# A hybrid mixer and mixture-of-experts step on one core: the first shift and scale from eight slabs of whole rows, x loaded first

## The chip, the cores and the metric

The kernel runs on one core of a Trainium2 chip. The core has TensorE (PE, matrix products), VectorE (DVE), ScalarE (ACT), GpSimd (POOL) and SyncE (SP, here used to start DMA transfers). The engines run on their own and wait for each other by semaphores. On-chip data lie in SBUF (128 partitions); TensorE writes into eight banks of PSUM. Weights come from device memory through 16 DMA engines, which serve queues that SP, ACT and POOL fill. The metric is the device time of one execution in microseconds (us); the runs of the kernel before gave 1415.63, 1417.6 and 1422.11 us, median 1417.6.

## The reference, cut to what matters

Two groups of 128 tokens (context and denoising sample, 1024 channels) go through one layer with shared weights. All in float32.

```python
mod = silu(cond) @ w_mod + b_mod                 # per group; six parts of 1024: sh1, sc1, g1, sh2, sc2, g2
h = rmsnorm(x) * norm1_g * (1 + sc1) + sh1       # first shift and scale; x_sample has pos added first
z = h @ w_in + b_in                              # 20 column slabs of 256: Fourier, conv a, conv b, S5, 3 gates
br_f = fourier_mix(z_f) @ w_four
br_c = silu(layernorm(depthwise_conv31(z_a * sigmoid(z_b)))) @ w_conv_out
br_s = glu(gelu(s5_scan_both_directions(z_s))) @ w_ssm_out
x = x + g1 * ((gate_f * br_f + gate_c * br_c + gate_s * br_s) @ w_out)
x = x + g2 * top4_of_32_experts(rmsnorm(x) * norm2_g * (1 + sc2) + sh2)
y = rmsnorm(x) * final_norm_g
```

The outputs are y for both groups and the final S5 states. The S5 parameters (lam, dt, B, C) are made into tables of complex powers first; the scan then goes over 16 chunks.

## The kernel before, in words

The weights come in slabs of 1 MB ([128, 2048] float32). A ring (class Ring, line 169) has a list of slabs in the order in which they are wanted and a list of free slots; when a slab is done with, its slot is given back and the next load is written into SP's queue (give and pump, lines 179 to 189). Slots 0 to 3 go round like this in the first part; slots 6 to 9 are dropped after their first use (line 440), because they become S5 tables.

The order of all instructions up to the router is made when the program is built: some thirty generators (line 1364) each yield one operation or the name of a flag that they wait for, and a planner (class Sched, line 55) always takes the operation that could start first by its own table of costs, plus 0.2 us for each point in PRIO. Each engine then runs its instructions in the order in which they were handed out. An in-order queue so can hold up work that is ready behind work that is not; this holds for SP's loads too. The planner's costs know nothing of two engines that slow each other.

The first shift and scale are made in four blocks of 256 channels. A slab m0 of this part (line 350) has all 1024 input rows of 256 output columns, of the shift or of the scale, so its rows in memory are 1 KB long; two slabs make a block. first_mod (line 497) multiplies the two conditions (cs, padded to 32 columns) with a slab, eight input chunks over four row groups of a bank, two chunks to each group. modulate (line 517) copies each block's bank out to R0, turns it by four transposes into PSUM, sums the four row groups (vsum, line 528), adds b_mod (line 529), makes (1 + sc1) * norm1_g (line 531), and applies both to xT, the transposed normalized x: on ScalarE rounded to hhi (line 536), on VectorE in full (line 538) and the rest as hlo (line 539). Each block sets flags hmod0 to hmod7 for the channels done.

Around it run: s5_params, s5_inputs and powers (VectorE steps on 128x32 pieces, from lam and dt; flags lam, Bb, pw0); b_transposes (from ssm_b_re and ssm_b_im, for Bb); first_norm (line 547, from X and pos); tables_in (line 803, 24 steps of 128x1024 for four tables T0 to T3, shared out between VectorE and POOL, from Bb and pw0); m1_transposes (line 810, the tables turned into slots 6 to 9); columns_in (line 442, seven late parameter loads on SP, begun at flag R0); splitter (line 1063, each weight slab in four pieces, ScalarE rounds, VectorE or POOL subtracts); main_products (line 1099, three products per pair, from flag m0 and hmod), two banks in turn; evacuate (line 1157, which waits for flag M11 before it writes the first S5 columns, since they share a table's buffer). The S5 scan (line 880) follows the tables, and the convolution's 31 taps (line 989) the eighth column slab. The expert stage loads 12 slabs for each of 32 experts through 20 slots.

The loads at the start stand at lines 420 to 440. "Y" is SP's queue, "S" ScalarE's, "G" POOL's.

Of the kernel before, what the change touches and what calls it, by code (L numbers as in the profile page):

```python
# [9 lines left out]
F32 = mybir.dt.float32  # L10
# [195 lines left out]
def build(tc, A, O):  # L206
# [3 lines left out]
    with es:  # L210
# [40 lines left out]
        def dma(e, dst, src):  # L251
            n = 1
            for d in dst.shape:
                n *= d
            return sch.op(f"{e}{n * 4 / 3.6e5:.3f}", 1.0 if e == "G" else 0.05, [dst] if local(dst) else [],
                          [src] if local(src) else [], lambda: ENG[e].dma_start(dst, src))
# [4 lines left out]
        def tr(out, in_):  # L261
            return sch.op("P", 0.107 * in_.shape[0] / 128, [out], [in_], lambda: te.transpose(out, in_, ident[:in_.shape[0], :in_.shape[0]]))  # L262

        def mm(out, lhsT, rhs, start, stop=False):
            n, m = size(rhs), lhsT.shape[1]
            if lhsT.dtype != F32:
                c = max(n, m) * 4.17e-4
            elif m > 64:
                c = max(n, m) * 1.667e-3
            else:  # L270
                c = n * 1.667e-3 / (4 if m <= 32 else 2) + 0.0145
            return sch.op("P", c, [out], [lhsT, rhs],
                          lambda: te.matmul(out, lhsT, rhs, start=start, stop=stop, skip_group_check=True))  # L273
# [10 lines left out]
        def stt(o, a, sc, b, op0=OP.mult, op1=OP.add, e="V"):  # L284
            c = size(o) * 1.05e-3 + (0.07 if len(o.shape) == 2 else 0.125)
            return sch.op(e, c, [o], [x for x in (a, sc, b) if hasattr(x, "tensor")],
                          lambda: ENG[e].scalar_tensor_tensor(o, a, sc, b, op0=op0, op1=op1))  # L287

        def tt(o, a, b, op=OP.mult, e="V"):
            c = size(o) * 1.05e-3 + 0.07 if e == "V" else size(o) * 1.85e-3 + 0.25  # L290
            return sch.op(e, c, [o], [a, b], lambda: ENG[e].tensor_tensor(o, a, b, op=op))  # L291
# [14 lines left out]
        def copy(o, a):  # L306
            return act(o, a, AF.Copy)
# [5 lines left out]
        def vsum(o, a):  # L313
            return sch.op("V", size(a) * 1.05e-3 + 0.06, [o], [a],
                          lambda: v.tensor_reduce(o, a, axis=mybir.AxisListType.X, op=OP.add))  # L315
# [26 lines left out]
        def add_cols(key, w, c0, n, K):  # L342
            ring.add(key, lambda sl: sl[:, :].rearrange("p (k c) -> p k c", k=K),
                     w[:, c0:c0 + n].rearrange("(k p) c -> p k c", p=128))

        for k in range(4):
            if k == 3:
                add_cols(("in", COLS[0]), A["w_in"][0], COLS[0], 256, 8)
            for i in range(2):
                add_cols(("m0", k, i), A["w_mod"][0], 1024 * i + 256 * k, 256, 8)  # L350

        def add_mod(b, i):

# [8 lines left out]
        n = 0  # L362
# [54 lines left out]
        def start(*slots):  # L417
            ring.free = [SL[x] for x in slots]
            ring.pump()
        dma("S", cst[:, 0:C_DFT], A["cst"][:, 0:C_DFT])  # L420
        for i, n in enumerate(("ssm_lam_re", "ssm_lam_im")):
            dma("Y", SR[:, i].rearrange("g (d p) -> g d p", d=2), A[n][0].rearrange("d g p -> g d p"))
        for d in range(2):
            dma("Y", dtl[d * 64:(d + 1) * 64], A["ssm_log_dt"][0, d:d + 1, :].to_broadcast([64, 32]))
        dma("S", crow[0:8], A["c_ctx"].rearrange("(k p) -> k p", p=128))
        dma("S", crow[8:16], A["c"][0].rearrange("(k p) -> k p", p=128))
        dma("Y", mrow[0:16], A["b_mod"][0, 0:2048].rearrange("(k p) -> k p", p=128))
        dma("Y", mrow[16:24], A["norm1_g"][0].rearrange("(k p) -> k p", p=128))
        dma("Y", X[:, 0], A["x_prompt"][0])
        dma("Y", X[:, 1], A["x_sample"][0])  # L430
        dma("Y", pos, A["pos"])
        for i, n in enumerate(("ssm_b_re", "ssm_b_im")):
            dma("Y", BR[i].rearrange("g d p h -> g d (p h)"), A[n][0].rearrange("d g p h -> g d (p h)"))
        start(0, 1)
        start(2, 3)
        start(6, 7, 8, 9)
        dma("G", vrow[0:40], A["b_in"][0].rearrange("(k p) -> k p", p=128))
        for i, n in enumerate(("conv_dw_b", "conv_ln_g", "conv_ln_b", "ssm_d", "b_ssm_glu")):
            dma("G", vrow[40 + 4 * i:44 + 4 * i], A[n][0].rearrange("(k p) -> k p", p=128))
# [18 lines left out]
        rs = sm.tile([128, 4, 2], F32, name="rs")  # L458
        xr = SL[22][:, :].rearrange("p (g d) -> p g d", g=2)
        xT = SL[20][:, :].rearrange("p (k g t) -> p k g t", k=8, g=2)  # L460
        R0 = [SL[15][:, 1024:1536], SL[15][:, 1536:2048]]
        modA = sm.tile([128, 2, 8, 2], F32, name="modA")
        pm = sm.tile([128, 4, 2], F32, name="pm")
        hhi = new(4, F32R)[:, :].rearrange("p (k t) -> p k t", k=8)
        hlo = new(5, F32R)[:, :].rearrange("p (k t) -> p k t", k=8)

# [30 lines left out]
        def first_mod():  # L497

            yield tr(PB[2][:, 0:16], crow[:, :])
            yield act(csg[:, :], PB[2][:, 0:16], AF.Sigmoid)  # L500
            yield tt(cs[:, :, 0:2].rearrange("p k g -> p g k"), PB[2][:, 0:16].rearrange("p (g k) -> p g k", g=2),
                     csg[:, :].rearrange("p (g k) -> p g k", g=2))
            for b in range(4):
                for i in range(2):
                    w = ring.get(("m0", b, i))[:, :].rearrange("p (k c) -> p k c", k=8)
                    for k in range(8):
                        q = 32 * (k % 4)
                        yield mm(PB[b % 2][q:q + 32, 256 * i:256 * i + 256], cs[:, k, :], w[:, k], k < 4 and i == 0, k >= 4)
                    ring.done(("m0", b, i))
                if b > 1:  # L510
                    yield f"P{b - 2}"
                yield copy(R0[b % 2], PB[b % 2][:, :])
                flags.add(f"R{b}")
            sch.stop("warm")
            flags.add("m0")

        def modulate():

            for b in range(4):
                yield f"R{b}"  # L520
                if b == 0:
                    yield tr(PB[2][:, 64:96], mrow)
                    yield copy(vec[:, 60:84], PB[2][:, 64:88])
                for i in range(4):
                    yield tr(PB[2][:, i * 128:(i + 1) * 128], R0[b % 2][:, i * 128:(i + 1) * 128])
                flags.add(f"P{b}")
                k2 = slice(2 * b, 2 * b + 2)
                yield vsum(pm[:, :, :], PB[2][:, :].rearrange("p (i q r) -> p i r q", i=4, q=4)[:, :, 0:2])
                yield tt(modA[:, :, k2], pm[:, :, :].rearrange("p (s k) g -> p s k g", s=2), vec[:, 60:76].rearrange("p (s k) -> p s k", s=2)[:, :, k2, None].to_broadcast(
                    [128, 2, 2, 2]), OP.add)  # L530
                yield stt(modA[:, 1, k2], modA[:, 1, k2], 1.0, vec[:, 76 + 2 * b:78 + 2 * b, None].to_broadcast([128, 2, 2]),
                          op0=OP.add, op1=OP.mult)
                yield f"xT{b}"
                for k in (2 * b, 2 * b + 1):
                    for g in range(2):
                        yield act(hhi[:, k, 128 * g:128 * g + 128], xT[:, k, g], AF.Identity, bias=modA[:, 0, k, g:g + 1],
                                  scale=modA[:, 1, k, g:g + 1])
                        yield ts(xT[:, k, g], xT[:, k, g], modA[:, 1, k, g:g + 1], modA[:, 0, k, g:g + 1])
                    yield tt(hlo[:, k], flat(xT[:, k]), fv(hhi[:, k]), OP.subtract)
                    flags.add(f"hmod{k}")  # L540
                if b == 3:
                    yield tr(PB[2][:, 0:64], vrow)
                    yield copy(vec[:, 0:60], PB[2][:, 0:60])
                    flags.add("vec")
            flags.add("h")

        def first_norm():
# [260 lines left out]
                flags.add(f"T{j}")  # L808

        def m1_transposes(js, banks):  # L810
            yield from need("xT", "R2", *(("m0",) if js[0] else ()))
            for j in js:
                if j == 2:
                    yield "in0"
                yield f"T{j}"
                for h in range(2):
                    for i in range(2):
                        for g in range(2):
                            for r in range(2):
                                yield tr(banks[i][:, (2 * g + r) * 128:(2 * g + r + 1) * 128], flat(M1T[j][r][:, 4 * h + 2 * i + g]))  # L820
                    for i in range(2):
                        yield copy(flat(M1[j][:, 4 * h + 2 * i:4 * h + 2 * i + 2]), banks[i][:, :])
                flags.add(f"M1{j}")
# [951 lines left out]
```

## Time and profile before

| What | Value |
|---|---|
| median of 3 runs | 1417.6 us (1415.63 to 1422.11) |
| profiled execution, its own time | 1418.22 us |
| span of its trace | 1416.4 us |
| busy: TensorE, VectorE, ScalarE, POOL | 1243.9, 492.4, 301.5, 216.0 us |
| read from device memory | 472.61 MB, 335 GB/s over the span |

The span runs from the first to the last instruction that the profiler saw. Busy shares are averages over stages that differ, so the sections below are read by stage: up to about 107 us preparation, up to 317.5 us scan and convolution beside the products, up to 378.3 us the last products and the router, then 32 experts. In a timeline row stand the start, the duration, the engine, the line in the kernel (that of a helper: 262 transposes, 273 products, 279 to 291 VectorE and POOL arithmetic, 304 ScalarE, 256 DMA starts), the operation, what it writes and reads, and in brackets how long the engine was idle before it and what ended that.

### The profile page before, as it was taken

Reading aid. Unit: us, or ns where it says so; the run is one execution under the profiler, and the core shown is the slowest. Engines: PE = TensorE matmul, PEld = TensorE weight load, DVE = VectorE, ACT = ScalarE, POOL = GpSimd, SP = SyncE. Lnnn points to the kernel's source line nnn. Section 1 sums busy time; section 2 is a strip of 40 time slices with the busy share of each in tenths; the row PEclk is TensorE's granted clock in tenths of the full one; section 3 lists DMA queues with packets and bytes.
Section 4 is the critical chain, followed back from the end, with each engine's and each line's share of the span. In section 5 each row is a group of like instructions: output and inputs, shape, how many; then the busy total and the mean of one; then the engine's idle time right before and its main releaser. Section 6 shows DMA issues by size and latency. Waiting matters only on the chain. (4 is left out here: it accounts for less than half of the span.)

```text
span 1416.4 us, 19588 instructions
## 1 busy us (share of the span) xinstructions
PE 1243.9 (88%) x7444; PEld 655.7 (46%) x7444; DVE 492.4 (35%) x839; ACT 301.5 (21%) x609; POOL 216.0 (15%) x183
## 2 busy tenths in 40 slices
PE   4596787899999999999989999999999989999994
PEld 3475686789833433334343433333334334343331
DVE  7949898897511111111111111111121111211113
ACT  4454344454311101011100101101011101111011
POOL 4555556565300000000000000000000000000001
PEclk9798899999999999999999999999999999999996
DMA  9563489558799999999998999998999994999990
GB/s 268 193 210 115 144 146 266 188 196 316 290 352 410 416 397 415 416 416 415 417 415 319 407 417 414 415 400 357 416 416 416 416 409 185 413 415 415 414 395 33
DMA packets 124834, 477.08 MB, mean 337 GB/s; under 512 B 11871, under 2 KB 49505, under 8 KB 90864
## 3 DMA queue, kind: packets, MB, share of 16 engines
q1 hardware_dynamic: 121744, 468.25, 85.3%
q0 software_dynamic: 2288, 5.76, 1.2%
q8 instruction: 120, 1.97, 0.6%
q10 hardware_dynamic: 624, 0.63, 0.1%
q14 instruction: 58, 0.48, 0.1%
HBM read 472.61 MB, written 1.61 MB: 335 GB/s over the span
## 5 line engine op out<-in xcount | busy, mean ns | idle before, releaser
L273 PE MATMUL pb<-sl,sl 128*64 128x512 f32 (+4 forms) x5344 | 951.3, 485 | 48.7 <-PEq L1644 13.1
L273 PEld LDWEIGHTS pb<-sl,sl 128*64 128x64 f32 (+2 forms) x5344 | 438.4, 152 | 521.8 <-issue 445.2
L304 ACT ACTIVATE sl<-sl 128x512 fp32r<-128x512 f32 (+4 forms) x211 | 120.8, 588 | 614.2 <-DVE sl L279 496.4
L291 POOL TENSOR_TENSOR sl<-sl,sl 128x512 fp32r<-128x512 f32 (+4 forms) x73 | 121.1, 1667 | 737.5 <-DVE sl L291 607.7
L279 DVE TENSOR_SCALAR sl<-pb 128x512 f32<-128x512 f32 (+1 forms) x35 | 23.7, 676 | 434.7 <-PE pb L273 434.7
L287 DVE SCALAR_TENSOR_TENSOR sl<-pb,wsl,sl 128x512 fp32r<-128x512 f32 x64 | 47.7, 750 | 310.5 <-ACT sl L304 309.3
L291 DVE TENSOR_TENSOR sl<-sl,sl 128x512 fp32r<-128x512 f32 (+3 forms) x107 | 105.6, 1001 | 30.1 <-ACT sl L304 27.7
L304 ACT ACTIVATE sl<-pb 128x512 f32<-128x512 f32 (+6 forms) x125 | 68.5, 585 | 199.2 <-PE pb L273 177.8
L262 PE MATMUL pb<-cst,sl 128*128 128x128 f32 (+2 forms) x354 | 57.4, 296 | 46.0 <-ACT sl L304 15.0
L304 ACT ACTIVATE sl<-pb,wsl 128x512 fp32r<-128x512 f32 x64 | 43.6, 687 | 199.6 <-PE pb L273 196.6
L273 PE MATMUL pb<-sl,PT 128*128 128x512 f32 x256 | 78.0, 428 | 0.5 <-PEq L1644 0.5
L273 PE MATMUL pb<-hb,sl 128*128 128x128 f32 x512 | 68.4, 289 | 7.9 <-DVE hb L291 7.5
L273 PEld LDWEIGHTS pb<-hb,sl 128*128 128x128 f32 x512 | 65.1, 200 | 18.3 <-ACT wsl L304 11.8
L262 PEld LDWEIGHTS pb<-cst,sl 128*128 128x128 f32 (+2 forms) x354 | 43.7, 158 | 63.0 <-issue 26.1
L318 POOL MEMSET sl<- 128x30 f32 (+6 forms) x15 | 2.8, 228 | 374.1 <-PEq L1644 373.8
L287 DVE SCALAR_TENSOR_TENSOR hb<-sl,taps,hb 128x256 f32<-128x256 f32 x90 | 55.5, 664 | 0.6
L273 PEld LDWEIGHTS pb<-sl,PT 128*128 128x128 f32 x256 | 46.2, 201 | 8.0 <-ACT sl L304 1.3
L291 POOL TENSOR_TENSOR sl<-PWT,sl 128x1024 f32<-128x1024 f32 x20 | 43.5, 2190 | 11.1 <-PE pb L273 6.2
L273 PEld LDWEIGHTS pb<-comb,hb 128*128 128x128 f32 x128 | 19.6, 207 | 44.6 <-DVE sl L279 41.9
L291 DVE TENSOR_TENSOR sl<-sl 128x512 f32<-128x512 f32 (+4 forms) x77 | 37.1, 500 | 4.1 <-ACT sl L304 0.5
L273 PE MATMUL pb<-comb,hb 128*128 128x1 f32 x128 | 22.0, 241 | 18.2 <-PEq L1644 16.4
L273 PE MATMUL pb<-ha,selb 128*64 128x512 bf16 (+1 forms) x140 | 21.3, 390 | 16.8 <-PEq L1644 14.4
(176 smaller groups left out, 547.0 us busy)
## 6 DMA issues: line engine op xcount, KB each, us to landing
sl<-w_gate_up SPq DMA_DIRECT2D x256, 1024.0 KB, 14.9
sl<-w_down SPq DMA_DIRECT2D x128, 1024.0 KB, 17.5
sl<-w_mod SPq DMA_DIRECT2D x24, 1024.0 KB, 7.2
sl<-w_in SPq DMA_DIRECT2D x20, 1024.0 KB, 11.1
sl<-w_out SPq DMA_DIRECT2D x4, 1024.0 KB, 6.9
sl<-md POOLq DMA_DIRECT2D x6, 512.0 KB, 6.9
sl<-w_four SPq DMA_DIRECT2D x2, 1024.0 KB
sl<-Kd SPq DMA_DIRECT2D x16, 128.0 KB, 9.2
```

What stands on the lines that cost most here:

```text
L262: return sch.op("P", 0.107 * in_.shape[0] / 128, [out], [in_], lambda: te.transpose(out, in_, ident[:in_.shape[0], :in_.shape[0]]))
L273: lambda: te.matmul(out, lhsT, rhs, start=start, stop=stop, skip_group_check=True))
L279: return sch.op(e, c, [o], ap, lambda: ENG[e].tensor_scalar(o, a, s1, None, op0=op0))
L287: lambda: ENG[e].scalar_tensor_tensor(o, a, sc, b, op0=op0, op1=op1))
L291: return sch.op(e, c, [o], [a, b], lambda: ENG[e].tensor_tensor(o, a, b, op=op))
L304: [a] + [x for x in (bias, scale) if hasattr(x, "tensor")], lambda: s.activation(o, a, func, **kw))
L318: return sch.op(e, size(o) * 0.9e-3 + 0.1, [o], [], lambda: ENG[e].memset(o, val))
```

## The change

- The eight m0 slabs are now 128 input rows each, all 2048 columns of shift and scale (rows of 8 KB in memory). All eight stand ahead of the first projection slab, and fill slots 0 to 3 and 6 to 9.
- All of them are summed over in one bank, by the helper adaln that the later parts use: four products of 512 columns for each slab, into four row groups.
- modulate waits for all eight, copies one block, turns it by four transposes, and adds b_mod to all channels at once. Then it applies shift and scale to xT as before. The transposes of mrow and vrow, and so the flag vec, come ahead of it.
- The flag R0, which starts columns_in, is set after the fifth slab. m1_transposes waits for m0 in both threads.
- The first loads: x, sample and pos lead SP's queue, then the eight slabs, then ssm_b_re and ssm_b_im. ScalarE's queue has c_ctx, c, the constants, lam and dt. POOL's has b_mod and norm1_g ahead of b_in and the others.

```diff
-        for k in range(4):
-            if k == 3:
-                add_cols(("in", COLS[0]), A["w_in"][0], COLS[0], 256, 8)
-            for i in range(2):
-                add_cols(("m0", k, i), A["w_mod"][0], 1024 * i + 256 * k, 256, 8)
+        for k in range(8):
+            ring.add(("m0", k), lambda sl: sl[:, :], A["w_mod"][0, k * 128:(k + 1) * 128, 0:2048])
+        add_cols(("in", COLS[0]), A["w_in"][0], COLS[0], 256, 8)
...
-        dma("S", cst[:, 0:C_DFT], A["cst"][:, 0:C_DFT])
-        for i, n in enumerate(("ssm_lam_re", "ssm_lam_im")):
-            dma("Y", SR[:, i].rearrange("g (d p) -> g d p", d=2), A[n][0].rearrange("d g p -> g d p"))
-        for d in range(2):
-            dma("Y", dtl[d * 64:(d + 1) * 64], A["ssm_log_dt"][0, d:d + 1, :].to_broadcast([64, 32]))
-        dma("S", crow[0:8], A["c_ctx"].rearrange("(k p) -> k p", p=128))
-        dma("S", crow[8:16], A["c"][0].rearrange("(k p) -> k p", p=128))
-        dma("Y", mrow[0:16], A["b_mod"][0, 0:2048].rearrange("(k p) -> k p", p=128))
-        dma("Y", mrow[16:24], A["norm1_g"][0].rearrange("(k p) -> k p", p=128))
         dma("Y", X[:, 0], A["x_prompt"][0])
         dma("Y", X[:, 1], A["x_sample"][0])
         dma("Y", pos, A["pos"])
+        dma("S", crow[0:8], A["c_ctx"].rearrange("(k p) -> k p", p=128))
+        dma("S", crow[8:16], A["c"][0].rearrange("(k p) -> k p", p=128))
+        dma("S", cst[:, 0:C_DFT], A["cst"][:, 0:C_DFT])
+        start(0, 1, 2, 3, 6, 7, 8, 9)
+        for i, n in enumerate(("ssm_lam_re", "ssm_lam_im")):
+            dma("S", SR[:, i].rearrange("g (d p) -> g d p", d=2), A[n][0].rearrange("d g p -> g d p"))
+        for d in range(2):
+            dma("S", dtl[d * 64:(d + 1) * 64], A["ssm_log_dt"][0, d:d + 1, :].to_broadcast([64, 32]))
         for i, n in enumerate(("ssm_b_re", "ssm_b_im")):
             dma("Y", BR[i].rearrange("g d p h -> g d (p h)"), A[n][0].rearrange("d g p h -> g d (p h)"))
-        start(0, 1)
-        start(2, 3)
-        start(6, 7, 8, 9)
+        dma("G", mrow[0:16], A["b_mod"][0, 0:2048].rearrange("(k p) -> k p", p=128))
+        dma("G", mrow[16:24], A["norm1_g"][0].rearrange("(k p) -> k p", p=128))
...
-            for b in range(4):
-                for i in range(2):
-                    w = ring.get(("m0", b, i))[:, :].rearrange("p (k c) -> p k c", k=8)
-                    for k in range(8):
-                        q = 32 * (k % 4)
-                        yield mm(PB[b % 2][q:q + 32, 256 * i:256 * i + 256], cs[:, k, :], w[:, k], k < 4 and i == 0, k >= 4)
-                    ring.done(("m0", b, i))
-                if b > 1:
-                    yield f"P{b - 2}"
-                yield copy(R0[b % 2], PB[b % 2][:, :])
-                flags.add(f"R{b}")
+            for k in range(8):
+                yield from adaln(("m0", k), PB[0])
+                if k == 4:
+                    flags.add("R0")
...
+            yield tr(PB[2][:, 64:96], mrow)
+            yield copy(vec[:, 60:84], PB[2][:, 64:88])
+            yield tr(PB[2][:, 96:160], vrow)
+            yield copy(vec[:, 0:60], PB[2][:, 96:156])
+            flags.add("vec")
+            yield "m0"
+            yield copy(R0, PB[0][:, :])
+            for i in range(4):
+                yield tr(PB[2][:, i * 128:(i + 1) * 128], R0[:, i * 128:(i + 1) * 128])
+            sums = PB[2][:, :].rearrange("p (i s j r) -> p s j i r", i=4, s=2, j=2)
+            for n in (1, 0):
+                yield tt(modA[:, n].rearrange("p (j i) g -> p j i g", j=2), sums[:, n, :, :, 0:2],
+                         vec[:, 60 + 8 * n:68 + 8 * n].rearrange("p (j i) -> p j i", j=2)[:, :, :, None].to_broadcast([128, 2, 4, 2]), OP.add)
+                if n:
+                    yield stt(modA[:, 1], modA[:, 1], 1.0, vec[:, 76:84, None].to_broadcast([128, 8, 2]), op0=OP.add, op1=OP.mult)
             for b in range(4):
-                yield f"R{b}"
...
-                for i in range(4):
-                    yield tr(PB[2][:, i * 128:(i + 1) * 128], R0[b % 2][:, i * 128:(i + 1) * 128])
-                flags.add(f"P{b}")
-                k2 = slice(2 * b, 2 * b + 2)
-                yield vsum(pm[:, :, :], PB[2][:, :].rearrange("p (i q r) -> p i r q", i=4, q=4)[:, :, 0:2])
...
                 yield f"xT{b}"
```

## Rows read from the trace of the kernel before

**Rows 1.** The page, busy tenths of VectorE in 40 equal slices of the span.
```profile
DVE  7949898897511111111111111111121111211113
```

**Rows 2.** Table of stretches: length, busy us (instructions) by engine, clock, DMA share, GB/s.
```profile
0.00:29.40 29.40, 10.66 (x78) 9.23 (x78) 21.16 (x112) 9.39 (x14) 8.97 (x19) 1.00 0.90 252
29.40:107.00 77.60, 62.92 (x513) 43.81 (x514) 58.59 (x68) 40.35 (x86) 44.50 (x28) 0.89 0.66 215
107.00:260.00 153.00, 114.67 (x1173) 102.07 (x1172) 140.74 (x221) 70.05 (x150) 86.29 (x64) 0.87 0.65 175
260.00:317.50 57.50, 51.22 (x403) 49.70 (x402) 50.78 (x68) 26.65 (x48) 34.71 (x34) 0.94 0.51 172
317.50:378.30 60.80, 58.37 (x480) 56.37 (x478) 39.37 (x57) 28.62 (x62) 29.42 (x27) 0.97 0.83 311
378.30:1399.30 1021.00, 943.61 (x4798) 393.19 (x4797) 169.76 (x297) 121.73 (x242) 6.22 (x9) 0.98 0.96 388
```

**Rows 3.** TensorE's waits in the expert stage, 378.3 to 1399 us: total, times, longest.
```profile
PE pb L273 <- PEq L1644: 44.4, 77, 0.7
...
PE pb L273 <- DMA sl<-w_gate_up: 3.6, 6, 0.7
```

**Rows 4.** Timeline of SP's queue, the first w_mod loads.
```profile
6.24 19.65 SPq L256 DMA_DIRECT2D sl<-w_mod  x6
```

**Rows 5.** Table of stretches, columns as in Rows 2, for loads.
```profile
10.00:16.00 6.00, 1.33 (x12) 1.34 (x13) 4.90 (x36) 1.15 (x2) 0.00 (x0) 1.00 1.05 149
16.00:26.00 10.00, 5.26 (x44) 4.83 (x43) 8.00 (x32) 2.05 (x2) 4.44 (x3) 1.00 1.10 349
440.00:460.00 20.00, 18.69 (x92) 6.14 (x87) 3.22 (x5) 2.00 (x3) 0.00 (x0) 1.00 1.02 416
```

**Rows 6.** Timeline: last m0 products, first main products, last modulated piece.
```profile
53.94 1.07 PE L273 MATMUL pb<-sl,cs 128*32 128x256 f32 x16
...
66.79 3.12 PE L273 MATMUL pb<-sl,sl 128*128 128x256 f32 x13
...
69.35 0.43 DVE L291 TENSOR_TENSOR sl<-sl,sl 128x256 fp32r<-128x256 f32 x1
```

**Rows 7.** Instruction groups by shape, 29.4 to 84.3 us: busy us, mean ns, idle before.
```profile
L291 POOL TENSOR_TENSOR sl<-PWT,sl 128x1024 f32<-128x1024 f32 x8 | 18.3, 2302 | 4.8 <-ACT PWT L304 4.8
...
L291 DVE TENSOR_TENSOR sl<-PWT,sl 128x1024 f32<-128x1024 f32 x8 | 13.5, 1705 | 0.0
...
L291 POOL TENSOR_TENSOR sl<-sl,sl 128x1024 f32<-128x1024 f32 x4 | 11.1, 2783 | 0.2
...
L282 DVE TENSOR_SCALAR sl<-sl,modA 128x128 f32<-128x128 f32 x16 | 10.1, 666 | 0.0
...
L291 DVE TENSOR_TENSOR sl<-sl,sl 128x256 fp32r<-128x256 f32 x8 | 5.0, 629 | 0.3
```

**Rows 8.** Timeline of the first 30 us: parameters, pos added, ssm_b, Bb, tables.
```profile
4.87 0.25 DVE L282 TENSOR_SCALAR sl<-dtl 128x32 f32<-128x32 f32 x1 [3.73 <-DMA dtl<-ssm_log_dt]
...
13.35 1.22 DVE L291 TENSOR_TENSOR sl<-sl,sl 128x1024 f32<-128x1024 f32 x1 [1.03 <-DMA sl<-pos]
...
14.66 1.84 PEld L262 LDWEIGHTS pb<-cst,sl 32*128 32x128 f32 x16 [8.98 <-DMA sl<-ssm_b_re]
...
23.29 1.32 POOL L291 TENSOR_TENSOR sl<-sl 128x512 f32<-128x512 f32 x1
...
29.44 5.84 POOL L291 TENSOR_TENSOR sl<-PWT,sl 128x1024 f32<-128x1024 f32 x2 [4.84 <-ACT PWT L304]
```

**Rows 9.** Timeline: POOL's wait, its last table step, first scan step, convolution's split.
```profile
72.51 1.28 POOL L291 TENSOR_TENSOR sl<-sl,sl 128x512 fp32r<-128x512 f32 x1 [11.76 <-ACT sl L304]
...
81.47 2.71 POOL L291 TENSOR_TENSOR sl<-sl,sl 128x1024 f32<-128x1024 f32 x1
...
107.11 0.28 DVE L291 TENSOR_TENSOR w<-A8i,s 128x128 f32<-128x128 f32 x1
...
315.61 1.94 DVE L291 TENSOR_TENSOR sl<-ha,sl 128x512 fp32r<-128x512 f32 x2 [0.76 <-ACT sl L304]
```

More of the change, by code (lines that the diff above doesn't have):

```diff
@@ L460, in build @@
         xT = SL[20][:, :].rearrange("p (k g t) -> p k g t", k=8, g=2)
-        R0 = [SL[15][:, 1024:1536], SL[15][:, 1536:2048]]
+        R0 = SL[15][:, 1024:1536]
         modA = sm.tile([128, 2, 8, 2], F32, name="modA")
-        pm = sm.tile([128, 4, 2], F32, name="pm")
         hhi = new(4, F32R)[:, :].rearrange("p (k t) -> p k t", k=8)
@@ L517, in modulate @@
         def modulate():
-            for b in range(4):
-                yield f"R{b}"
-                if b == 0:
-                    yield tr(PB[2][:, 64:96], mrow)
-                    yield copy(vec[:, 60:84], PB[2][:, 64:88])
-                for i in range(4):
-                    yield tr(PB[2][:, i * 128:(i + 1) * 128], R0[b % 2][:, i * 128:(i + 1) * 128])
-                flags.add(f"P{b}")
-                k2 = slice(2 * b, 2 * b + 2)
-                yield vsum(pm[:, :, :], PB[2][:, :].rearrange("p (i q r) -> p i r q", i=4, q=4)[:, :, 0:2])
[L529 to L532, printed above, removed]
+            yield tr(PB[2][:, 64:96], mrow)
[13 more added lines that the diff above has]
+                    yield stt(modA[:, 1], modA[:, 1], 1.0, vec[:, 76:84, None].to_broadcast([128, 8, 2]), op0=OP.add, op1=OP.mult)
+            for b in range(4):
                 yield f"xT{b}"
@@ L540, in modulate @@
                     flags.add(f"hmod{k}")
[L541 to L544, printed above, removed]
             flags.add("h")
@@ L810, in m1_transposes @@
         def m1_transposes(js, banks):
-            yield from need("xT", "R2", *(("m0",) if js[0] else ()))
+            yield from need("xT", "m0")
             for j in js:
-                if j == 2:
-                    yield "in0"
                 yield f"T{j}"
```

## Prediction

> **What bounds the kernel now.** I read the page first, then a table of stages, then the waits of TensorE, and only then the first 110 us in order of time. The page's slices show VectorE nearly full for the first quarter with one dip [rows 1]. The table of stages [rows 2] cuts the span at what the program does: up to 29.4 us parameters and the first norm, up to 107 us modulation, tables and the first products, up to 317.5 us the S5 scan and the convolution (both on VectorE) beside the products, up to 378.3 us the last products and the router, then the experts. The reader should see which engine is full in which row. VectorE is busy 140.7 of 153 and 50.8 of 57.5 us in the third and fourth row (91%); TensorE 58.4 of 60.8 us in the fifth (96%) and 943.6 of 1021 us in the sixth (92%). In the expert stage TensorE's largest wait is its own branches, 44.4 us, and its wait for weights is 3.6 us [rows 3]. So nothing behind 317.5 us has slack, and a shift of the convolution's end and of the products in front of it goes to the end one for one. What can give is ahead of that: between 29.4 and 107 us VectorE is idle 77.6 - 58.6 = 19.0 us, and between 29.4 and 260 us TensorE is idle (77.6 - 62.9) + (153 - 114.7) = 53.0 us [rows 2]. The time of the profiled run is 1418.2 us, its span 1416.4, 0.6 us over the median of 1417.6; the sum is made against 1418.2.
>
> **The change, part by part.**
>
> *Loads of x and of the eight slabs.* Today six slabs are issued from 6.24 us on and take 3.3 us each [rows 4], at 349 GB/s, after a stretch of 149 GB/s in which the small ssm_b rows move [rows 5]. The expert slabs, whose rows are as long as the new ones (8 KB), move at 416 GB/s [rows 5]. After: x goes first. The loads of x, sample and pos are 1.57 MB; with the first data some 2.5 us behind the issue at 0.74 and 349 GB/s they are in at about 7.4 us. Eight slabs of 1.049 MB at 416 GB/s are 20.2 us, so the last lands near 27.6 us, and its matmuls take 1.07 us (the sixteen of today's last slab [rows 6]; the new ones are half as many and twice as wide, so no change): 28.7 us against 55.0 us. At 349 GB/s the eight take 24.0 us and the end is 32.5; both ends stay in the range, I take 416 because the row length is that of the expert slabs. The Trainium skill, "DMA: Bandwidth & Descriptors", Specifications, puts the share of HBM for one core at about 358 GB/s. By that figure the eight slabs would be an estimated 23.4 us, 3.2 us longer; the measured 416 GB/s disagrees, and I go by it.
>
> *Shift and scale.* Removed: three of four copies out of the bank, twelve transposes' worth of repeats (one group of four stays) and, on VectorE, twelve small steps (sum, add, scale-add, four of each) for which three stay. Undisturbed they are near 0.17 us each, so nine less are 1.5 us of VectorE. Then come the 24 VectorE steps on 128x128 and 128x256 pieces, which stay: 16 at 0.67 and 8 at 0.63 us [rows 7], 15.1 us, drawn out by POOL's table work beside them. They now fall between about 30.5 and 40 us, where POOL has little to do. I count no gain for that, because POOL's 29.4 us of table work (18.3 + 11.1 [rows 7]) must then lie beside something else on VectorE; the bounds are 0 and 6 us.
>
> *The products.* The first product runs at 66.8 us, and the last modulated piece is done at 69.8 us [rows 6]. After, the first projection slab is issued behind the eight and the ssm_b loads, lands near 35 us, and products begin at about 37 us; the third slab waits for the second table transposes, near 62 us. That wait is for a table buffer which the third slab's evacuation order needs. TensorE thus has its first products 25 to 30 us sooner, which is within its 53 us of idleness.
>
> *Loads moved back.* ssm_b_re and ssm_b_im now stand behind eight slabs on SP's queue. Today their data come at 14.7 us [rows 8], the last piece of Bb is done at 23.29 + 1.32 = 24.6 us, 10 us later, and the tables begin at 29.4 us, held by the powers and not by Bb [rows 8]. After, they land at 27.6 plus 3.5 us (0.52 MB at 149 GB/s), about 31 us, Bb ends near 41 us, and the tables begin there: 11.7 us later. In that gap VectorE does the modulation (30.5 to 40 us), so the gap itself is only some 2 us. POOL finishes its last table step at 84.2 us now [rows 9], but it sat idle for 11.8 us up to 72.5 us and again before 76 us, on ScalarE's copies [rows 9]; from 41 us on, 29.4 us of tables and 6 us of splits end near 78 us. The scan, first at 107.1 us [rows 9], comes with it at about 101.
>
> *Parameter loads on ScalarE's queue.* lam and dt are issued third to seventh there instead of first on SP. VectorE's first parameter step starts at 4.87 us, right after dt [rows 8]. With 3 issues in front, at 0.4 to 0.6 us, dt lands near 7 us: 2.1 us later. If the slabs crowd it, it could be as late as the ssm_b rows are today after issue, 9 us, that is 13 us; behind ScalarE's issues nothing waits but its first small copies. b_mod and norm1_g go to POOL's queue, ahead of b_in and five more: those come 1 us later and are first needed at the vec transposes, which wait for nothing then. The seven column loads are now given out after the fifth slab, all together, where today they stand between slabs that wait for TensorE; they cost the next slab some 5 us of queue, covered by three slabs already in.
>
> *Sum.* VectorE's idle time from 29.4 to 107 us falls from 19.0 us to about 7 (2 us before the tables, the rest waits for copies on ScalarE): -12.0. Nine small steps less: -1.5. dt later: +2.1. Together -11.4 us, all of it ahead of 317.5 us where VectorE sets the pace: 1418.2 - 11.4 = 1406.8 us, about 1407.
>
> **The rivals.**
>
> *The gain is used up before 317.5 us.* VectorE is idle another 12.3 and 6.7 us in the next two stages, waiting for ScalarE and TensorE [rows 2], and the order of work is a planner's: with a different start it deals the splits, the taps and the scan out differently. If what is won turns into such waits, the end moves by less than 7 us either way, to 1411 to 1425. For it: the last two stages hang on one late step, the convolution's split at 315.6 us [rows 9]. Against it: the convolution needs the seventh and eighth slab, and these come sooner.
>
> *The tables set the pace, and the end is late.* Place: Bb behind the eight slabs. Price: the 11.7 us by which the tables start later. If the scan, the kernel table and the last transposes follow that start with today's spacing (29.4 to 107.1 us), because POOL and VectorE do as many splits in between as today, the scan starts at 119 us and the time is 1418.2 + 11.7 = 1430 us. It decides once POOL's last table step ends later than today's 84.2 us. For it: VectorE's steps of 1024 take 1.22 us alone [rows 8] and 1.71 us beside POOL [rows 7], and with splits of three slabs ready at 41 us the two engines collide more. The Trainium skill, "SBUF — State Buffer", Who interferes with whom, calls the port pair of these two engines an exclusive lock; by it, each POOL step could hold up a VectorE step wholly, and the 1.71 against 1.22 agrees in kind. Against it: the modulation's 15 us no longer stand between the tables.
>
> *The change does more than that.* If also the 6 us of drawn-out modulation and half of the idle time behind 107 us go, 1418.2 - 11.4 - 6 - 9 = 1392 us.
>
> *It doesn't do what it says.* If SP gives the eight slabs out no faster than 3.3 us each, the last lands at 34 us instead of 27.6, still 20 us ahead of today; this costs up to 6 of the 11.4 us and lies in the first rival's span.
>
> **How the numbers follow.** Forecast (1399 to 1411): 0.45; the larger gain: 0.07; used up (1411 to 1425): 0.24; tables late: 0.24. About 0.5%, 7 us, is what a measurement of this kernel can tell from no change. Faster by over 7 us: 0.45 + 0.07 = 0.52; within: 0.24; slower: 0.24. The range leaves out most of the larger gain and the far half of the late tables: 1393 to 1427. The forecast's own range is 1399 to 1411.
>
> **What would show it.** Right: w_mod issues end near 25 us; the last first-modulation matmul near 29; the sixteen ScalarE steps that read modA between 30 and 40; the first 128x256 product near 37; the first 1024-wide table step near 41 and POOL's last near 78; the scan near 101; the convolution's split near 305; the first expert weights issued some 11 us before today's. Wrong: tables that end after 84 us; VectorE as idle between 30 and 107 us as today; a convolution split that stays at 315 us though the products came sooner; or an expert stage whose length changes.

## The result, and the profile after

The kernel after takes 1438.4 us (median of 4 runs, 1436.25 to 1442.83) against 1416.62 us before: ratio 1.0159, 95% interval 1.0135 to 1.0183, so some 22 us slower. Forecast were 1407 us, within 1393 to 1427. The profiled execution spans 1437.5 us.

The page after, VectorE and the granted TensorE clock in 40 slices. Beside [rows 1], the full stretch of VectorE has moved right by a slice, and it begins with a 2.

```profile
DVE  2874999788541111111112112121111202111114
PEclk9669989888999999999999999999999999999997
```

The table of stretches after, cut and columns as in [rows 2].

```profile
0.00:29.40 29.40, 16.27 (x99) 7.80 (x99) 7.23 (x30) 7.44 (x11) 5.35 (x16) 0.99 0.94 345
29.40:107.00 77.60, 44.95 (x264) 30.10 (x264) 58.47 (x126) 28.47 (x60) 41.88 (x32) 0.65 0.58 188
107.00:260.00 153.00, 114.96 (x1205) 100.28 (x1205) 129.26 (x197) 70.51 (x145) 89.64 (x47) 0.91 0.50 126
260.00:317.50 57.50, 49.70 (x367) 45.32 (x368) 47.87 (x71) 30.08 (x60) 35.27 (x41) 0.87 0.69 226
317.50:378.30 60.80, 50.73 (x399) 49.23 (x399) 45.91 (x64) 27.28 (x49) 31.48 (x31) 0.92 0.71 259
```

Read the third number after the comma, VectorE. In the first 29.4 us it is busy 7.23 us in place of 21.16, with 30 instructions in place of 112. The next row is as before (58.47 against 58.59), so its idle time there is 19.1 us as it was, not the 7 forecast. By 317.5 us VectorE has done 242.8 us of work; before it had done 271.3.

The loads came nearly as forecast. The table of stretches for loads (compare [rows 5]):

```profile
10.00:16.00 6.00, 1.53 (x6) 1.24 (x7) 4.23 (x21) 2.74 (x5) 0.00 (x0) 1.00 1.00 389
16.00:26.00 10.00, 10.00 (x60) 3.05 (x62) 1.59 (x9) 2.27 (x4) 0.00 (x0) 1.00 1.02 428
26.00:40.00 14.00, 8.02 (x43) 2.94 (x35) 0.94 (x9) 1.12 (x4) 0.00 (x0) 0.60 1.04 314
```

DMA issues of the first 40 us: destination and source, queue, count, KB, median us from issue to landing.

```profile
sl<-ssm_b_im SPq DMA_DIRECT2D x1, 256.0 KB, 21.3
...
dtl<-ssm_log_dt ACTq DMA_DIRECT2D x2, 8.0 KB, 4.2
...
sl<-ssm_lam_im ACTq DMA_DIRECT2D x1, 16.0 KB, 4.4
```

Timeline of ScalarE's queue, the issue of dt:

```profile
3.07 1.17 ACTq L256 DMA_DIRECT2D dtl<-ssm_log_dt  x2
```

So lam and dt are on the chip by some 8 us. Now see when they are used. VectorE's timeline: first step on dt, first step on L (the transposed lam), first step of the shift.

```profile
14.89 0.17 DVE L282 TENSOR_SCALAR sl<-dtl 128x32 f32<-128x32 f32 x1
...
33.42 0.29 DVE L291 TENSOR_TENSOR sl<-L,sl 128x32 f32<-128x32 f32 x2 [15.60 <-ACT L L304]
...
39.47 0.17 DVE L291 TENSOR_TENSOR modA<-pb,vec 128x16 f32<-128x16 f32 x1 [5.64 <-PE pb L262]
```

Its waits up to 107 us (total, times, longest):

```profile
DVE sl L291 <- ACT L L304: 15.6, 1, 15.6
DVE sl L291 <- DMA sl<-pos: 7.7, 1, 7.7
DVE modA L291 <- PE pb L262: 5.6, 1, 5.6
```

The longest wait names ScalarE, which copied L out of PSUM at 33.17 us. Behind that stands TensorE. Its timeline:

```profile
30.44 1.93 PE L273 MATMUL pb<-sl,cs 128*32 128x512 f32 x8 [3.40 <-DMA sl<-w_mod]
...
32.71 0.42 PE L262 MATMUL pb<-cst,sl 32*128 32x32 f32 x2
34.63 1.93 PE L273 MATMUL pb<-sl,cs 128*32 128x512 f32 x8 [1.50 <-DMA sl<-w_mod]
```

The two 32x32 transposes at 32.71 us turn lam. Before, they ran at 2.67 us. They now stand in TensorE's queue behind the products of the slabs, each of which waits for its slab; so lam, which landed at about 7 us, is first touched at 32.71. VectorE's first step on dt is late as well, 14.89 us against 4.87 [rows 8]: it stands behind the first norm.

What follows, in the timeline of several engines: first table step on VectorE, first scan step, first store of the S5 kernel table, TensorE's wait for that table, the convolution's split.

```profile
73.29 4.09 DVE L291 TENSOR_TENSOR sl<-PWT,sl 128x1024 f32<-128x1024 f32 x2 [0.80 <-ACT PWT L304]
...
142.40 1.05 DVE L291 TENSOR_TENSOR w<-A8i,s 128x128 f32<-128x128 f32 x1
...
229.47 2.69 SPq L256 DMA_DIRECT2D Kd<-sl  x6
...
260.42 2.00 PE L273 MATMUL pb<-sl,sl 128*32 128x128 f32 x22 [6.58 <-DMA sl<-Kd]
...
343.13 1.29 DVE L291 TENSOR_TENSOR sl<-ha,sl 128x512 fp32r<-128x512 f32 x2 [0.76 <-ACT sl L304]
```

Against 29.42 (POOL's first table step is at 29.44 [rows 8]), 107.11 [rows 9], 186.71, 219.82 and 315.61 us [rows 9] these are 43.9, 35.3, 42.8, 40.6 and 27.5 us late. The router's choice comes at 406.83 in place of 381.72 us, 25.1 late, and the span is 21.1 us longer.

### The profile page after: what moved, and what is told of

It reads as the page before. It is cut to its first block, busy times and chain, and to the rows that moved or that the text cites. A ratio compares the mean times of both kernels' runs of the same rounds, so it can differ in the third digit from the quotient of the medians.

```text
span 1437.5 us, 19402 instructions
## 1 busy us (share of the span) xinstructions
PE 1248.1 (87%) x7360; PEld 649.3 (45%) x7360; DVE 481.6 (34%) x830; ACT 301.7 (21%) x606; POOL 226.5 (16%) x185
## 5 line engine op out<-in xcount | busy, mean ns | idle before, releaser
L273 PE MATMUL pb<-sl,sl 128*64 128x512 f32 (+3 forms) x5344 | 955.5, 486 | 74.5 <-DVE sl L291 23.7
L304 ACT ACTIVATE sl<-sl 128x512 fp32r<-128x512 f32 (+5 forms) x211 | 120.8, 588 | 610.2 <-DVE sl L279 495.7
L291 POOL TENSOR_TENSOR sl<-sl,sl 128x512 fp32r<-128x512 f32 (+4 forms) x73 | 116.8, 1608 | 735.6 <-DVE sl L291 604.1
L291 DVE TENSOR_TENSOR sl<-sl,sl 128x512 fp32r<-128x512 f32 (+3 forms) x107 | 99.1, 938 | 43.9 <-ACT sl L304 35.4
L262 PE MATMUL pb<-cst,sl 128*128 128x128 f32 (+2 forms) x342 | 54.3, 293 | 41.1 <-DVE sl L291 25.0
L291 POOL TENSOR_TENSOR sl<-PWT,sl 128x1024 f32<-128x1024 f32 x20 | 46.4, 2339 | 17.5 <-PE pb L273 13.8
L273 PE MATMUL pb<-sl,cs 128*32 128x512 f32 (+1 forms) x256 | 33.5, 589 | 10.0 <-DMA sl<-w_mod 9.2
L291 POOL TENSOR_TENSOR hb<-hb,sl 128x256 f32<-128x256 f32 x30 | 35.1, 1169 | 25.5 <-ACT sl L304 24.5
```

Source lines behind the costliest of these rows:

```text
L304: [a] + [x for x in (bias, scale) if hasattr(x, "tensor")], lambda: s.activation(o, a, func, **kw))
```

## The experiments

Theory A: the order handed out. In the program the eight slabs stand ahead of the loads of lam and dt. The planner books all transfers on one server, in the order in which they are named; so by its book lam comes behind the slabs, though on the chip it has a queue of its own. It therefore hands lam's transposes out behind the slabs' products. Theory B: ssm_b behind the slabs. Theory C: one block in place of four.

**e1_lam_first** (four lines moved; each queue has the same loads in the same order).

```diff
-        start(0, 1, 2, 3, 6, 7, 8, 9)
         for i, n in enumerate(("ssm_lam_re", "ssm_lam_im")):
             dma("S", SR[:, i]...)
         for d in range(2):
             dma("S", dtl[...], ...)
+        start(0, 1, 2, 3, 6, 7, 8, 9)
```

> The changed kernel, with the four lines that start the lam and dt loads ahead of the line that starts the eight slabs. Both queues keep their order (ScalarE's and SP's), so the loads on the chip are the same; only the planner's book of when lam and dt arrive differs, and with it the order of instructions. Theory A (the order handed out is the cause: lam's transposes stand behind the slabs' products on TensorE): first parameter step on VectorE near 8 us instead of 33, tables from about 41 us instead of 73, time 1405 to 1418 us. Theory B (ssm_b behind the slabs): tables no sooner than about 60 us, time within 5 us of 1438. Theory C (one block instead of four): within 5 us of 1438.

Measured: 1420.76 us (10 runs), ratio to before 1.003 (1.0014 to 1.0046). ScalarE's copy of L in its timeline:

```profile
7.75 0.22 ACT L304 ACTIVATE L<-pb 128x64 f32<-128x64 f32 x1
```

The loads kept their queues and their order there, and 17.6 of the 22 us came back. Theory A has the cause right and its sizes too good: the tables start at 58.4 us, not 41, and the time is 2.8 us above its range and still 2.0 to 6.5 us above before. The tables' place is near what B said; e3 below, with ssm_b first, starts them at 32.9.

**h1_lam_mid** (lam and dt named between the fourth and the fifth slab), run last.

```diff
-        start(0, 1, 2, 3, 6, 7, 8, 9)
+        start(0, 1, 2, 3)
         (lam and dt, as in the kernel after)
+        start(6, 7, 8, 9)
```

> The kernel after with the four lines of lam and dt between the fourth and the fifth slab (each hardware queue still has the same loads in the same order). Theory A (the planner books them behind the slabs named ahead of them, and hands the parameter chain out by that book): lam's copy L comes between 7.8 us (e1_lam_first) and 33.2 us (the kernel after), near 20, and the time lies between their 1420.8 and 1438.4, near 1430 if each slab in front costs alike. Rival: what costs is the loads' true place on the queues or the single block, and the kernel stays within 3 us of the kernel after.

Measured: 1429.0 us (4 runs), ratio 1.0078 (1.0051 to 1.0106), halfway. L in ScalarE's timeline:

```profile
23.48 0.22 ACT L304 ACTIVATE L<-pb 128x64 f32<-128x64 f32 x1 [1.73 <-PE pb L262]
```

So more slabs named ahead cost more. The way of the cost is not the one that I would have drawn: the tables start at 58.3 us, as in e1 (58.4), and the scan at 124.4 against 119.9. The rest of the 8 us is lost later (the convolution's split ends at 328.3 against 318.7); which step loses it stays open.

**e2_before_lam_late** (the kernel before, this one move alone).

```diff
         (the first loads)
-        dma("Y", lam), dma("Y", dt)   # first on SP's queue
...
         start(0, 1); start(2, 3); start(6, 7, 8, 9)
+        dma("S", lam), dma("S", dt)   # same four loads, on ScalarE's queue
```

> The kernel before, with only the lam and dt loads moved: to ScalarE's queue and behind the slabs in the program, as the change has them. Slabs, blocks, x and ssm_b as before. Theory A: the parameter chain starts some 25 us later and the time rises by 12 to 25 us, to 1429 to 1442. Theories B and C: within 4 us of before, since neither ssm_b nor the blocks are touched.

Measured: 1444.31 us (4 runs), ratio 1.0195 (1.0158 to 1.0231). L in ScalarE's timeline:

```profile
39.68 0.20 ACT L304 ACTIVATE L<-pb 128x64 f32<-128x64 f32 x1
```

The move of lam and dt alone makes the kernel before 28 us slower, without new slabs, 2 us more than A's range. The new queue is not what delays it: lam is issued at 2.11 and 2.48 us and lands 3.7 us later. That shows A from the other side.

**e3_lam_b_first** (e1 with ssm_b ahead of the slabs too).

```diff
+        (the two loads of ssm_b)
         start(0, 1, 2, 3, 6, 7, 8, 9)
-        (the two loads of ssm_b)
```

> As the run with lam first, and ssm_b_re and ssm_b_im too ahead of the eight slabs on SP's queue. Theory A: against the run with lam first, tables start 5 to 12 us sooner, and the time is 0 to 8 us lower. Theory B: this run alone recovers, to 1410 to 1420 us, while lam first doesn't. Theory C: within 5 us of 1438.

Measured: 1419.8 us (10 runs), ratio 1.0015 (0.9993 to 1.0037). The tables start at 32.9 us in place of 58.4, and the end moves by 1 us, within the intervals. The 1419.8 lies in B's range too, but B asked that e1 should not recover, and e1 had. An early start of the tables is not worth its distance here: they share VectorE with the modulation, whose last step ends at 72.2 us and in e1 at 53.0.

**e4_slabs_only** (slabs and arithmetic of the kernel after, first loads in the order of the kernel before).

```diff
+        (cst, lam, dt, c, b_mod, norm1_g as before, ahead)
         dma("Y", X[:, 0], ...); dma("Y", X[:, 1], ...); dma("Y", pos, ...)
         (ssm_b as before, ahead)
         start(0, 1); start(2, 3); start(6, 7, 8, 9)
```

> The eight whole-row slabs, summed in one bank and applied in one block, as in the change, with all first loads in the order of the kernel before. Theory A: the parameter chain starts near 5 us as before, and the time is 1405 to 1420. Theory B: the same as A here (ssm_b lands ahead of the slabs). Theory C: 1432 to 1442, as slow as the change.

Measured: 1414.55 us (10 runs), ratio 0.9988 (0.9968 to 1.0008). Against before that is 4.5 us less to 1.1 us more. So the slabs and the one block together cost nothing, and C falls; a gain like the forecast 11 us is not there either. That opens the second question: where the forecast gain goes even when lam is early. In e4 the scan ends 9.5 us sooner than before (156.9 against 166.4), the first store of the S5 kernel table comes 0.5 us sooner, and the router's choice at 381.7 us, as before. The scan starts no sooner (107.5 against 107.1 us), it is shorter: before, POOL's table steps lie beside its last part (147.9 to 163.8 us), and two of its 128x128 steps fill 4.44 us at 159.49; in e4 POOL is idle from 145.6 to 157.3 us.

Two things seem to take the lead back. First, VectorE's groups at 155 to 182 us (busy us, mean ns), before:

```profile
L291 DVE TENSOR_TENSOR sl<-sl,sl 128x512 fp32r<-128x512 f32 x12 | 9.8, 831 | 1.9 <-ACT sl L304 1.9
...
L279 DVE TENSOR_SCALAR sl<-sl,cst 128x512 f32<-128x512 f32 x4 | 1.7, 479 | 0.0
```

and in e4:

```profile
L291 DVE TENSOR_TENSOR sl<-sl,sl 128x512 fp32r<-128x512 f32 x8 | 11.4, 1432 | 1.5 <-ACT sl L304 1.5
...
L279 DVE TENSOR_SCALAR sl<-sl,cst 128x512 f32<-128x512 f32 x4 | 3.8, 1000 | 0.0
```

Steps of the same shape take 1.7 and 2.1 times as long, and POOL's last table steps now lie beside them. That they are the cause is read from the overlap; no run takes them away. POOL's timeline in e4 (before, it worked next to nothing from 164 to 181 us):

```profile
164.98 2.39 POOL L291 TENSOR_TENSOR sl<-PWT,sl 128x1024 f32<-128x1024 f32 x1
...
169.04 2.39 POOL L291 TENSOR_TENSOR sl<-PWT,sl 128x1024 f32<-128x1024 f32 x1
171.51 2.69 POOL L291 TENSOR_TENSOR sl<-sl,sl 128x1024 f32<-128x1024 f32 x1
```

Second, the table's trip through device memory: 16 stores, then 16 loads, for which TensorE stands in order. TensorE's timeline, before:

```profile
219.82 0.64 PE L273 MATMUL pb<-sl,sl 128*32 128x128 f32 x4 [5.28 <-DMA sl<-Kd]
```

and in e4:

```profile
220.01 2.31 PE L273 MATMUL pb<-sl,sl 128*32 128x128 f32 x32 [10.96 <-DMA sl<-Kd]
```

TensorE arrives 5.5 us sooner and leaves at the same time. A lead of this size in one trace proves little: before, f1 and f4 have the same order of instructions up to the trip, and their scans start at 107.1, 106.4 and 102.1 us. So the medians must decide. Theory D: this trip takes the lead. Rival F: the convolution on VectorE sets the end anyway. Four runs test this:

```diff
-            (16 stores RS, R7 -> Kd; 16 loads Kd -> M3)
+            two loads of 1 MB of w_gate_up into M3; the planner's book unchanged     # f1, f2, f3
+            (the 16 stores to a spare table Kz first, then all as before)            # f4
```

**f1_before_short_trip**

> The kernel before with the trip of the S5 kernel table through device memory cut short: the 16 stores are left out and the 16 loads are replaced by two loads of 1 MB of other data into the same buffer (this leaves out the table's contents). Theory D (TensorE stands in order for the table's trip at 219.8 us, and this sets everything behind it): the wait of 5.28 us goes, and the time falls by 5 to 12 us against the kernel before, to 1404 to 1411. Rival F (the convolution's taps on VectorE set the end of the stage, the wait is filled in anyway): within 3 us of the kernel before, 1413 to 1419.

Measured: 1414.55 us (10 runs), ratio 0.999 (0.9969 to 1.0011). **F holds here**: TensorE waits for VectorE a little later instead.

```profile
227.16 1.23 PE L273 MATMUL pb<-sl,sl 128*128 128x256 f32 x4 [5.34 <-DVE sl L291]
```

**f2_slabs_short_trip**

> The same short trip in e4_slabs_only (the slabs of the kernel after, the first loads in the order of the kernel before). It ran 4 to 7 us ahead of the kernel before at 167 to 215 us and level with it from 222.7 us on. Theory D: the lead of some 5 us is kept once the trip no longer sets the order, so the time falls by 9 to 16 us, to 1399 to 1406, and stands some 5 us under f1_before_short_trip. Rival F: within 3 us of e4_slabs_only (1414.6), and level with f1_before_short_trip.

Measured: 1407.35 us (5 runs), ratio 0.9923 (0.9892 to 0.9954): 7 us under e4 and under f1. **D holds here**: by the ratio 10.9 us under before, of 9 to 16 forecast, with the median 1.35 us above its range. The same wait for VectorE is over 2.5 us sooner:

```profile
224.62 1.65 PE L273 MATMUL pb<-sl,sl 128*128 128x256 f32 x6 [5.71 <-DVE sl L291]
```

So the short trip is worth 7 us with the new slabs and about 1 without them, and with it the new slabs are 7 us ahead. Not all of that is work done sooner. In the profiled runs (f1's is the slowest of its ten) only 2.5 us are there by the router (376.2 against 378.7 us). Some 3 us more are one idle of TensorE near the end of the expert stage, as its timeline shows in f1:

```profile
1390.00 1.01 PE L262 MATMUL pb<-cst,sl 128*128 128x128 f32 x4 [5.69 <-issue]
```

and in f2:

```profile
1379.00 1.08 PE L262 MATMUL pb<-cst,sl 128*128 128x128 f32 x4 [2.29 <-DVEq L1589]
```

This idle is 5.0 to 5.7 us in all five profiled kernels with the old slabs and 2.1 to 3.0 us in all nine with the new ones. What makes it is not shown; it stands in every comparison of old slabs with new, that of e4 with before too.

**f3_lam_first_short_trip**

> The same short trip in e1_lam_first. TensorE waited 10.57 us for the table there. Theory D: the time falls by 9 to 14 us against e1_lam_first (1420.8), to 1407 to 1412. Rival F: within 3 us of e1_lam_first.

Measured: 1416.07 us (10 runs), ratio 0.9999 (0.9985 to 1.0013), 4.7 us under e1; D asked for 9 at least and F for 3 at most, so neither holds. Its scan starts 15.3 us after that of f2, and TensorE waits 18.3 us for VectorE's splits at 160 to 420 us (f2: 9.1).

**f4_before_long_trip**

> The kernel before with the trip made longer: the 16 stores of the table are issued a second time, first to a spare table, then to the true one (some 9.5 us more on SyncE's queue; nothing is left out). Theory D: the wait at 219.8 us grows by 7 to 10 us, and the time rises by as much, to 1423 to 1426. Rival F: within 3 us of the kernel before.

Measured: 1423.24 us (10 runs), ratio 1.004 (1.0018 to 1.0061). TensorE's wait in its timeline:

```profile
222.92 5.25 PE L273 MATMUL pb<-sl,sl 128*32 128x128 f32 x67 [13.70 <-DMA sl<-Kd]
```

The wait grows from 5.28 to 13.7 us, but 5.3 of these 8.4 us come from an earlier arrival in this execution (209.2 against 214.5 us); TensorE goes on 3.1 us later than before. The end is 6 us later by the ratio (2.5 to 8.6), somewhat less than D's 7 to 10. The trip is near the limit in the kernel before: longer costs, shorter does not pay.

Last, two tries to use this. In e4 the 16 loads move 2 MB at 98 GB/s (196 to 218 us), and the planner books 360.

```diff
-        dma("Y", M3[a][...], Kd[...])
+        dma("Y", M3[a][...], Kd[...], rate=0.98e5)     # bytes per ms, in place of 3.6e5; g1 and g4
```

**g1_slabs_trip_booked**

> e4_slabs_only with one figure of the planner changed: the table's 16 loads are booked at 98 GB/s, the rate that the trace shows at 196 to 218 us, in place of 360 (nothing is left out). The planner then hands six ready products of 128x256 (some 0.3 us each) out ahead of the ones that wait for the table. Theory D (the table's trip gives back the lead of the slabs): the work taken out from behind the wait is worth 2 us, up to 6 if the order behind it gets better too, so 1409 to 1413. Rival: the trip itself, and not what stands behind it, sets the end, so a better order brings nothing: within 2 us of e4_slabs_only (1414.6).

Measured: 1413.48 us (10 runs), ratio 0.9982 (0.997 to 0.9995). That is 1 us under e4, in the rival's range, and not told apart from e4. It is the one full kernel here whose interval lies under before, by 0.7 to 4.2 us, which the 3 us of late idle could make alone. TensorE still waits 11.1 us for the table. The order behind changed much: the convolution's split ends 20 us sooner (297.4), and TensorE is full up to the router, whose choice comes at 383.7 us, no sooner than in e4. The table of stretches shows it:

```profile
317.50:378.30 60.80, 60.38 (x504) 59.44 (x503) 31.21 (x44) 30.58 (x64) 29.81 (x25) 0.98 0.82 304
```

**g4_before_trip_booked**

> The kernel before with the same figure of the planner changed as in g1_slabs_trip_booked (nothing is left out). Its trip is worth 1 to 3 us at most by f1_before_short_trip, so both theories expect it within 3 us of the kernel before; a gain as in g1 here would say that the order behind the trip, and not the slabs, is what g1 shows.

Measured: 1418.76 us (10 runs), ratio 1.0026 (1.0006 to 1.0045): no gain, and 0.8 to 6.4 us slower, at the edge of what both expected. A convolution that is 20 us sooner brings nothing once TensorE has its products still to do.

**g2_lam_b_first_short_trip**

> e3_lam_b_first with the short trip of f2_slabs_short_trip (this leaves out the table's contents). f3_lam_first_short_trip stayed 8.7 us above f2_slabs_short_trip, with its scan 15.3 us later (124.5 against 109.2). Theory B again, hidden so far by the trip: loading ssm_b behind the slabs does cost, once the trip gives nothing back; this kernel's scan starts at 108.2 as in f2, so it comes out at 1406 to 1410. Rival: the slabs ahead of everything cost by themselves; it stays near f3, 1413 to 1417.

Measured: 1411.84 us (10 runs), ratio 0.997 (0.9953 to 0.9988): between the two expectations, with its scan at 112.5 and not 108.2 us, so it decides nothing. The price of ssm_b behind the slabs stays open between 0 and some 4 us.

## Why the prediction was wrong

**The step that failed is "Parameter loads on ScalarE's queue".** It priced the move by the landing of the load (dt near 7 us, +2.1 us) and looked at what stands behind the issues on ScalarE. The landing was right. What it left out is the order of TensorE and VectorE, which the planner makes from the place of the load in the program: lam's transposes went from 2.67 to 32.71 us, and VectorE's first step on dt to 14.89 us, not near 7. The term was not 2.1 but 18 us (e1 against after) to 28 us (e2). That the planner serves all transfers from one book could be read in the kernel.

**"VectorE's idle time falls from 19.0 to 7", -12.0.** It did not fall in any version: 19.1 us after, 20.4 in e1, 23.4 in e4. The sum names none of the waits that were to end. I took TensorE's early products as work for VectorE, but the tables and the modulation share it, and what one gains the other waits for. With the order repaired, this and the other terms came to 0 within the measurement (e4), not to -11.4. This is the first rival, the gain used up before 317.5 us, and with lam repaired its 1411 to 1425 holds (e4, 1414.55). Where it goes is shown for the table's trip by e4 against f2, and only read from the overlap for the steps beside POOL.

**The slabs.** 428 GB/s at 16 to 26 us against 416 forecast: right. The last slab's products start at 34.63 us, not near 27.6. One part is x: 0.74 + 2.5 + 4.5 is 7.75 us, not the 7.4 of the sum, and the step that waits for pos starts at 8.86. Then the rate falls to 314 GB/s at 26 to 40 us, where the ssm_b rows (issued at 13.29 and 15.76 us) move too. TensorE is busy 11.0 of 11.0 us at 16 to 27 us at a granted clock of 1.00 (2.4 GHz), then waits 3.4 us for a slab, and the clock is 0.50 (1.2 GHz) at 30.4 to 41 us: eight products of 128x512 take 1.93 us where the same eight took 1.06 at 25.72.

**Shift and scale.** The ScalarE steps that read modA run from 40.0 to 49.2 us: 9 us long as forecast, 9 us late. I gave no gain for VectorE's steps outside POOL's table work; they take 461 and 425 ns in place of 666 and 629 [rows 7], together 4.9 us, near the bound of 6. The Trainium skill, "SBUF — State Buffer", Who interferes with whom, calls the port pair that VectorE and POOL share an exclusive lock. The 831 against 1432 ns at 155 to 182 us agree in kind.

**The rival "tables late"**, 1430 us, had the right side and the wrong cause. Its place was Bb behind the slabs; e3 took that away for 1 us. Its rule, that the scan follows the tables' start, fails too: in e3 the tables start 25.5 us before those of e1, and the scan 11.8 us.

**The end.** Behind 317.5 us a shift goes through nearly whole, as forecast: 27.5 us at the split, 25.1 at the router, 21.1 in the span. Of the last 4 us, 3.1 are the late idle of TensorE (5.54 us before, 2.42 after). But the convolution's end alone does not set the rest: in g1 and g4 its split ends 20 us sooner, and the router's choice comes at 383.7 and 382.4 us, not before 381.7.

## What to carry to other kernels

Where a program orders its engines when it is built, the place of a load in the text is a statement to the planner, beside a place on a queue: move a load only after asking where its readers will then stand on in-order engines, and look at the first reader, not at the landing. Read the first microseconds after a change for an engine that waits for data long on the chip. And before a lead is counted as a gain, look for a chain behind it that does not start sooner, here a trip through device memory, and a second engine that will now work beside the steps that became early. A lead of 5 us in one trace is no more than two executions of one kernel can differ by; let the medians decide.

## What the runs showed of the hardware

- One core's loads of 8 KB rows moved at 428 GB/s for 10 us (after, 16 to 26 us).
- ssm_b_im, 256 KB on 32 partitions, took 21.3 us from issue to landing behind the eight slabs on the same queue (after). dt, 8 KB on ScalarE's queue, took 4.2 us while x and pos moved on SP's.
- Loads of the S5 kernel table in rows of 512 bytes filled the DMA engines (share 1.14 at 196 to 218 us in e4) at 98 GB/s.
- The clock granted to TensorE was 0.65 in the mean from 29.4 to 107 us after the change (0.89 before, [rows 2]), where it was busy 44.95 of 77.6 us (62.92 before).
